# A macaron hybrid block on one core: the opening's order written out further, weight buffers kept for blocks, activation sums split late

## The chip, the cores and the metric

The kernel runs on one core of one Trainium2 chip. The metric is the device time of one execution in microseconds (us), as the median of several runs; less is better. TensorE (PE) multiplies matrices and holds a stationary operand that a separate weight load (PEld) brings in; ScalarE (ACT) and VectorE (DVE) work element by element; SyncE (SP) only issues the DMAs of the weights here.

## The reference

One layer over x of 256 positions by 2048 features, in float32: a half-step SwiGLU FFN, a token mixer of two head groups, a second half-step FFN, and a final norm.

```python
def swiglu_ffn(x, w_gate, w_up, w_down):
    return (jax.nn.silu(x @ w_gate) * (x @ w_up)) @ w_down
...
x = x + 0.5 * swiglu_ffn(rms_norm(x, ffn1_norm), ffn1_w_gate, ffn1_w_up, ffn1_w_down)
z = rms_norm(x, mix_norm) @ w_in
...
x = x + y @ w_out
x = x + 0.5 * swiglu_ffn(rms_norm(x, ffn2_norm), ffn2_w_gate, ffn2_w_up, ffn2_w_down)
return rms_norm(x, final_norm)
```

The FFN's inner width is 5632 (11 chunks of 512), the mixer reads 5120 columns of w_in. All weights are float32 and are read once: 340 MB. The change touches the two FFNs only.

## The kernel before

**Three matmuls for one.** TensorE's operands are fp32r. Each float32 operand is kept as two parts, hi (the value rounded by a cast on ScalarE) and lo (the rest, a subtraction on VectorE), and a product is hi·hi + lo·hi + hi·lo. A *unit* is a weight tile of 512 rows by 512 columns (1 MB, 128 partitions by 4 by 512). `unit` (L207) loads it into a raw buffer, casts it in two halves (`hi`, two ACT instructions of 128x1024) and subtracts (`lo`, one DVE instruction of 128x2048). `multiply` (L214) runs the unit against the activations of both position tiles: 16 matmuls with the hi part, then 8 with the lo part.

**Seven products for eight.** `seven` (L379) computes a block of two row units by two column units of a weight with seven products of 12 matmuls (Strassen's scheme in Winograd's form); the remaining rows of the block are `usual` units of 24. The weight sums of the scheme (w11 = w12 − w11, then w22 − w11, and so on) are VectorE subtractions in place, in the raw buffers; a product's own hi and lo parts are made from the sum. The activations' sums are made once for each set of blocks by `seven_of` (L349): four sums of which each is split into hi and lo, numbered 4, 5, 6 and 2 by the product that uses them. The products run in the order 0, 4, usual, 5, usual, 6, 2, usual, 3, usual, 1. After the first two, `snap` copies their banks to SBUF on ScalarE (s1, s5), after the third and fourth again (u2, u3).

**An FFN.** `ffn` (L440) first multiplies the first 512 columns of gate and up unit by unit, while it normalises the activations. Then come five steps s, each with one gate and one up block of 1024 columns (`seven` at L761 and L763). After steps 0, 2 and 4, `down` (L686) turns the hidden chunks made so far into an update of the residual: a `product` of plain units for output columns 0 (c = 0), the sums of the hidden activations by `seven_of`, a `seven` block for columns 1 and 2, and a `product` for columns 3. The first of these has three row units, the others four. So there are six down blocks and twelve down products in the two FFNs.

**What sets the order.** Each engine executes its own queue in order. The queues are laid out at build time by the tile framework's planner: it goes through the instructions in program order, and where the next one isn't ready by its own reckoning, it takes a later one that is. An instruction issued through the `Engine` wrapper (L32) while `Engine.pinned` is true is kept behind the pinned ones before it on its engine; later ones that aren't pinned may still pass it. The opening of the first FFN (`begin`, L561, the first 512 columns of gate and up while x and the weights come in) is pinned and written out by hand, and the pin holds on until `meanwhile(0)` (L753), that is, until s1 and s5 of the first gate block are issued. SP's queue is kept in program order (`sp.held`) through that first block.

**The opening.** x comes in by chunks of 512 columns, the first in two halves. Two norm-free activation units are made first: each 128 columns of x are turned by TensorE (`norm.turn`, two transposes), scaled and cast by ScalarE, subtracted by VectorE. The first gate unit comes in four quarters; `products(j)` (L586) is the quarter's six matmuls. In the loop of L595 each pass issues a turning, the quarter's cast and subtraction, and the products of the pass before. Five idle matmuls stand ahead of it (`keep_busy(5)`, two weight loads each), and two more behind the first transposed vector.

**Buffers.** Weight tiles come into three `raw` buffers (L179) or two `kept` ones (L177). The kept ones hold w11 and w12 of a block (L389). In the first FFN's steps and from there on, two of every five plain units of the down products take a kept buffer too (L173 to L175). Split tiles (hi and lo) have two sets and a third for every third unit. Thirteen small `keep` tiles hold the copies and the activation sums.

Of the kernel before, what the change touches and what calls it, by code (L numbers as in the profile page):

```python
# [13 lines left out]
ALU = mybir.AluOpType  # L14
# [35 lines left out]
def hybrid_block(ctx: ExitStack, tc: tile.TileContext, a: dict, out: bass.AP):  # L50
# [52 lines left out]
    early = const.tile([P, 1], F32, name="early")  # L103
    act.activation(early, ones[:, :1], AF.Copy, scale=1.0)

# [29 lines left out]
    first_turn()  # L135
    keep_busy(2)
    pe.held = False
# [31 lines left out]
    extra = []  # L169
    turn_of = {"raw": 0, "split": 0, "hold": False}  # L170

    def load(src, name, pieces=((0, UK),), loaded=None, kept=False):
        if kept is None and extra and not turn_of["hold"]:  # L173
            turn_of["raw"] += 1
            kept = turn_of["raw"] % 5 > 2  # L175
        if kept:
            raw = extra[0].tile([P, UK, CW], F32, tag="kept", name=f"raw_{name}", bufs=2)  # L177
        else:
            raw = raws.tile([P, UK, CW], F32, tag="raw", name=f"raw_{name}")  # L179
        for i, e in pieces:  # L180
            sp.dma_start(raw[:, i:e, :], src[i * P : e * P].rearrange("(j p) c -> p j c", p=P))
            if loaded:
                loaded(i)
        return raw
# [22 lines left out]
    def unit(src, name):  # L207
        return parts_of(load(src, name, kept=None), name)

# [22 lines left out]
    class Norm:  # L232
# [4 lines left out]

        def squares(self, c):
            for t in range(NT):
# [109 lines left out]
    def seven_of(sf, x0, x1, v, spare, parts):  # L349

        a11, a12, a21, a22 = v[0, 0], v[0, 1], v[1, 0], v[1, 1]
        parts = iter(parts)

        def split(i, q):
            hi, lo = next(parts)
            act.copy(hi, q)
            dve.tensor_tensor(lo, q, f32(hi), op=ALU.subtract)
            sf[i] = [(hi[:, j, :], lo[:, j, :]) for j in range(UK)]  # L360

        sf.update({0: stationary(x0, 0), 1: stationary(x1, 0), 3: stationary(x1, 1)})
        dve.tensor_tensor(spare, a21, a22, op=ALU.add)
        split(4, spare)
# [9 lines left out]
        return rest  # L374

    def quad(tile):
        return tile.rearrange("p (j c) -> p j c", j=UK)

    def seven(w, rows, cols, sf, xs, name, keep, done, between=None):  # L379

# [38 lines left out]
        product_of(5, w11, a)  # L419
# [20 lines left out]
    def ffn(tag, norm, after, opening=False):  # L440
        with tc.tile_pool(name=f"ffn{tag}", bufs=1, side="left") as fp:
            extra.append(fp)
            turn_of["hold"] = True
            wg, wu, wd = (a[f"ffn{tag}_w_{s}"][0] for s in ("gate", "up", "down"))
# [87 lines left out]
            def sums():  # L532
# [5 lines left out]
                else:  # L538
                    left.pop()()

# [15 lines left out]

            def joint(u, m, blk, middle=None, late=None):
                x = norm.xT[u] if u < 2 else units[u]
                multiply([(ps[m, t], stationary(x, t), u == 0, u % 2 == 1) for t in range(NT)], blk, True, middle, late)

            def begin():  # L561
# [16 lines left out]

                def mm(u, m, middle=None, late=None):
                    joint(u, m, blocks(*parts[u, m]), middle, late)  # L580

# [34 lines left out]
                high(1, "g")  # L616
                norm.squares(1)
                norm.squares(2)
                low(1, "g", ends)
                plain(1)  # L620
                mm(1, "g")
# [12 lines left out]
                mm(1, "u", norm.rows, lambda: turn_both(2))  # L634
                low(2, "g")
# [46 lines left out]
            if not opening:  # L682
                first_hidden()
            turn_of["hold"] = False

            def down(last):  # L686
# [10 lines left out]
                for c in (0, 3):  # L697
# [8 lines left out]
                    if c == 0:  # L706
                        sh = {}
                        seven_of(
                            sh, hidden[m], hidden[n],
                            {(t, i): turned[u, t] for t in range(NT) for i, u in ((0, m), (1, n))},  # L710
                            quad(keep(f"hspare{tag}_{m}")),
                            [[quad(keep(f"hs{tag}_{m}_{i}_{z}", F32R)) for z in range(2)] for i in range(4)],
                        )()
                        got = {}
# [7 lines left out]
                        if tag == 1 and m == 5:  # L722
                            prepare()
                        seven(wd, (m, n), (2 * CW, CW), sh, [(u, hidden[u]) for u in us[:-2]], f"d{tag}_{m}", keep, add)
                hidden.clear()
                turned.clear()

            for s in range(5):
# [31 lines left out]

                seven(wg, (0, 1), cs, sf, xs, f"g{tag}_{s}", keep, gate, meanwhile)  # L761
                sp.held = False
# [348 lines left out]
```

## Time and profile before

| | us |
|---|---|
| median of 3 runs | 1738.01 |
| lowest and highest | 1737.01, 1739.35 |
| the profiled execution's own time | 1736.9 |
| its span, first to last instruction | 1735.1 |
| TensorE busy, matmuls | 1721.8 |
| VectorE busy | 1477.9 |
| ScalarE busy | 1046.9 |

The profile is one execution; its times count from the start of the span. A row of the timeline has the start, the length from the first to the last of a run of like instructions, the engine, the source line (nearly all are L43, the wrapper's, so one goes by the tile names), the operation, out<-in, the shape, how many, and in brackets the engine's idle time before it and what ended it. The names: raw, hi and lo with _g, _u, _d for gate, up and down, with _p in a product of the seven, with _x in a usual unit; xs and hs are the split activation sums, ps the banks. PEld rows are weight loads; one precedes each matmul.

### The profile page before, as it was taken

To read this page: it belongs to the slowest core of one execution; us is meant where nothing else is said; L and a number is where in the kernel's file an instruction comes from. 1 tells how busy PE (TensorE), PEld (TensorE's weight loads), DVE (VectorE), ACT (ScalarE), POOL (GpSimd) and SP (SyncE) were. 2 spreads that over 40 slices of the span, in tenths; PEclk is the share of its full clock that TensorE was granted. 3 is DMA by queue.
4 is the path that set the end of the run, shared out by engine and by line. 5 is a ranking of instruction groups with operands and counts; after the bars stand their busy time and mean duration, and the time that the engine had idled before them with its cause. 6 is when DMAs were issued, how large, how long until landed. Compare 5 with 4: busy or idle time off the path is not lost. (4 is left out here: it accounts for less than half of the span.)

```text
span 1735.1 us, 20339 instructions
## 1 busy us (share of the span) xinstructions
PE 1721.8 (99%) x8045; PEld 1437.0 (83%) x8045; DVE 1477.9 (85%) x1213; ACT 1046.9 (60%) x1354; POOL 6.9 (0%) x32
## 2 busy tenths in 40 slices
PE   9999999999999999999999999999999999999998
PEld 7788888888888888888888888888888888888886
DVE  7998989889789888687986669989799887899895
ACT  8666565656466656565655546656556664556654
POOL 1000000000000000000000000000000000000000
PEclk9999999999999999999999999999999999999999
DMA  8663665666466656555555763575475646555743
GB/s 281 209 225 136 217 220 193 198 239 218 149 212 204 205 182 213 174 169 194 180 186 187 246 210 130 195 242 189 166 251 195 214 143 225 194 194 195 255 172 107
DMA packets 174224, 343.24 MB, mean 198 GB/s; under 512 B 5684, under 2 KB 8624, under 8 KB 174000
## 3 DMA queue, kind: packets, MB, share of 16 engines
q1 hardware_dynamic: 173632, 340.81, 58.2%
q8 instruction: 63, 1.03, 0.2%
q10 hardware_dynamic: 176, 1.06, 0.1%
q14 instruction: 33, 0.27, 0.0%
q0 software_dynamic: 320, 0.07, 0.0%
HBM read 339.82 MB, written 2.10 MB: 197 GB/s over the span
## 5 line engine op out<-in xcount | busy, mean ns | idle before, releaser
L43 ACT CAST hi_g_p<-raw_g 128x1024 fp32r<-128x1024 f32 x140 | 142.5, 1050 | 104.3 <-DVE raw_g L43 27.3
L43 DVE TENSOR_TENSOR lo_g_p<-raw_g,hi_g_p 128x2048 fp32r<-128x2048 f32 x70 | 159.4, 2287 | 33.4 <-ACT hi_g_p L43 33.3
L43 ACT CAST hi_u_p<-raw_u 128x1024 fp32r<-128x1024 f32 x140 | 141.2, 1049 | 69.9 <-PE ps_u_a L43 24.4
L43 DVE TENSOR_TENSOR lo_u_p<-raw_u,hi_u_p 128x2048 fp32r<-128x2048 f32 x70 | 159.1, 2286 | 18.8 <-ACT hi_u_p L43 18.5
L43 PE MATMUL ps_d<-hi_d,h 128*128 128x512 f32 x704 | 168.0, 390 | 0.0
L43 PEld LDWEIGHTS ps_d<-hi_d,h 128*128 128x128 f32 x704 | 131.5, 188 | 27.0
L43 PE MATMUL ps_in<-xT_nm,hi_in 128*128 128x512 f32 x640 | 153.3, 391 | 0.0
L43 PEld LDWEIGHTS ps_in<-xT_nm,hi_in 128*128 128x128 f32 x640 | 117.4, 188 | 23.2 <-ACT tha L43 0.3
L43 ACT CAST hi_d<-raw_d 128x1024 fp32r<-128x1024 f32 x88 | 88.3, 1049 | 67.9 <-PE ps_u_d L43 22.4
L43 DVE TENSOR_TENSOR lo_d<-raw_d,hi_d 128x2048 fp32r<-128x2048 f32 x44 | 100.6, 2291 | 30.8 <-ACT hi_d L43 30.8
L43 DVE TENSOR_TENSOR lo_in<-raw_in,hi_in 128x2048 fp32r<-128x2048 f32 x40 | 91.4, 2286 | 39.1 <-ACT hi_in L43 38.5
L43 ACT CAST hi_in<-raw_in 128x1024 fp32r<-128x1024 f32 x80 | 80.0, 1045 | 67.4 <-PE ps_in L43 45.9
L43 ACT CAST hi_d_p<-raw_d 128x1024 fp32r<-128x1024 f32 x84 | 84.4, 1048 | 51.7 <-DVE raw_d L43 39.4
L43 ACT CAST hi_g_x<-raw_g 128x1024 fp32r<-128x1024 f32 x80 | 81.3, 1048 | 49.6 <-PE ps_g_c L43 24.8
L43 DVE TENSOR_TENSOR lo_d_p<-raw_d,hi_d_p 128x2048 fp32r<-128x2048 f32 x42 | 95.4, 2287 | 11.9 <-ACT hi_d_p L43 11.8
L43 ACT CAST hi_u_x<-raw_u 128x1024 fp32r<-128x1024 f32 x80 | 80.5, 1047 | 34.1 <-PE ps_u_c L43 20.2
L43 DVE TENSOR_TENSOR raw_u<-raw_u,raw_u 128x2048 f32<-128x2048 f32 x40 | 91.6, 2289 | 8.6 <-DMA raw_u<-in_ffn_w_up_dram 8.0
L43 DVE TENSOR_TENSOR raw_g<-raw_g,raw_g 128x2048 f32<-128x2048 f32 x40 | 91.4, 2288 | 8.2 <-DMA raw_g<-in_ffn_w_gate_dram 7.6
L43 DVE TENSOR_TENSOR lo_g_x<-raw_g,hi_g_x 128x2048 fp32r<-128x2048 f32 x40 | 91.4, 2286 | 7.1 <-ACT hi_g_x L43 6.9
L43 DVE TENSOR_TENSOR lo_u_x<-raw_u,hi_u_x 128x2048 fp32r<-128x2048 f32 x40 | 91.4, 2285 | 1.1 <-ACT hi_u_x L43 1.0
L43 PE MATMUL ps_d<-lo_d,h 128*128 128x512 f32 x352 | 87.3, 389 | 0.0
L43 PEld LDWEIGHTS ps_in<-xT_nm,lo_in 128*128 128x128 f32 x640 | 82.1, 191 | 3.1
(363 smaller groups left out, 3565.4 us busy)
## 6 DMA issues: line engine op xcount, KB each, us to landing
raw_d<-in_ffn_w_down_dram SPq DMA_DIRECT2D x88, 1024.0 KB, 5.1
raw_u<-in_ffn_w_up_dram SPq DMA_DIRECT2D x87, 1024.0 KB, 5.2
raw_g<-in_ffn_w_gate_dram SPq DMA_DIRECT2D x86, 1024.0 KB, 5.3
raw_in<-in_w_in_dram SPq DMA_DIRECT2D x40, 1024.0 KB, 5.1
raw_o<-in_w_out_dram SPq DMA_DIRECT2D x16, 1024.0 KB, 5.1
xres<-in_x_dram SPq DMA_DIRECT2D x3, 512.0 KB, 9.4
raw_g<-in_ffn_w_gate_dram SPq DMA_DIRECT2D x4, 256.0 KB, 5.8
raw_u<-in_ffn_w_up_dram SPq DMA_DIRECT2D x2, 512.0 KB, 8.1
```

The costliest lines, as they stand in the source:

```text
L43: ins = getattr(self.engine, name)(*args, **kwargs)
```

## The change

Six edits:

1. The first ScalarE instruction is a Sqrt instead of a Copy; two idle matmuls are gone.
2. The opening's loop issues the quarter products in pairs, after every second turning. x's second chunk is loaded behind the second half of the first up unit, its third behind the second gate unit.
3. In the three units that follow, casts, subtractions and squares go by halves in another order, and the hi matmuls run over the first two row groups of both position tiles ahead of the last two. The turning of x's second chunk moves inside the first up unit (`within`).
4. The pin of the opening reaches to u2, the copy behind the first gate block's third product. The last two pairs of activation sums are made at written places in that block: the sums behind the first product's parts, the splits of 5 and 6 around w11's first sum, the last sum and split 2 behind u2. There, w22 − w11 is issued ahead of the usual unit (`early`).
5. Plain units take `raw` buffers only.
6. In the down blocks, only sum and split 5 are made ahead of the block. Split 6, the last sum and split 2 come behind the third product's weight sum, ahead of its parts.

```diff
-    act.activation(early, ones[:, :1], AF.Copy, scale=1.0)
+    act.activation(early, ones[:, :1], AF.Sqrt)
...
-    keep_busy(2)
...
     def load(src, name, pieces=((0, UK),), loaded=None, kept=False):
-        if kept is None and extra and not turn_of["hold"]:
-            turn_of["raw"] += 1
-            kept = turn_of["raw"] % 5 > 2
...
-        return parts_of(load(src, name, kept=None), name)
+        return parts_of(load(src, name), name)
...
-    def multiply(targets, blk, apart=False, middle=None, late=None):
+    def multiply(targets, blk, apart=False, middle=None, late=None, pieces=(range(UK),), within=None):
...
-        for ps, st, begin, _ in targets:
-            for j in range(UK):
-                pe.matmul(ps, st[j][0], blk[j][0], start=begin and j == 0, stop=False, **more)
-                pe.matmul(ps, st[j][1], blk[j][0], start=False, stop=False, **more)
+        for js in pieces:
+            for i, (ps, st, begin, _) in enumerate(targets):
+                if within and js is pieces[-1] and i == len(targets) - 1:
+                    within()
+                for j in js:
+                    pe.matmul(ps, st[j][0], blk[j][0], start=begin and j == 0, stop=False, **more)
+                    pe.matmul(ps, st[j][1], blk[j][0], start=False, stop=False, **more)
...
+        def high(i):
+            hi, lo = parts[i]
+            act.copy(hi, quads[i])
             sf[i] = [(hi[:, j, :], lo[:, j, :]) for j in range(UK)]
+        def low(i):
+            hi, lo = parts[i]
+            dve.tensor_tensor(lo, quads[i], f32(hi), op=ALU.subtract)
-        def rest():
+        def two():
             dve.tensor_tensor(a21, a11, a21, op=ALU.subtract)
             dve.tensor_tensor(a11, spare, a11, op=ALU.subtract)
-            split(5, a11)
-            split(6, a21)
+        def last():
             dve.tensor_tensor(a12, a12, a11, op=ALU.subtract)
-            split(2, a12)
...
         product_of(0, w11, a, True)
+        if between:
+            between("first")
         dve.tensor_tensor(w11, w12, w11, op=ALU.subtract)
+        if between:
+            between("first sum")
         product_of(4, w11, c, True)
         s1 = snap(a, "s1")
         s5 = snap(c, "s5")
         if between:
             between(0)
+        if early:
+            dve.tensor_tensor(w11, w22, w11, op=ALU.subtract)
         usual(0, b2, 1, (e, 1, True, not two), (c, 0, False, False))
         if between:
             between(1)
-        dve.tensor_tensor(w11, w22, w11, op=ALU.subtract)
+        if not early:
+            dve.tensor_tensor(w11, w22, w11, op=ALU.subtract)
+        if between:
+            between("sum")
         product_of(5, w11, a)
...
                     norm.turn((j,))
                     high(0, "g", quarters[j : j + 1])
                     low(0, "g", quarters[j : j + 1])
-                    if j:
+                    if j % 2:
                         products(j - 1)
-                products(UK - 1)
-                fetch(0, "u", ends, lambda i: load_x(1) if i == 0 else None)
+                        products(j)
+                fetch(0, "u", ends)
+                load_x(1)
+                fetch(1, "g", ends)
                 load_x(2)
-                fetch(1, "g", ends)
                 load_x(3)
-                high(0, "u")
-                his, los = turn(1)
-                his()
-                norm.squares(0)
-                low(0, "u", ends)
-                los()
-                plain(0)
-                mm(0, "u")
+                js = (range(2), range(2, UK))
+                high(0, "u", ends[:1])
+                norm.squares(0, (0,))
+                low(0, "u", ends[:1])
+                high(0, "u", ends[1:])
+                norm.squares(0, (1,))
+                low(0, "u", ends[1:])
+                def second():
+                    his, los = turn(1)
+                    his()
+                    los()
+                mm(0, "u", None, None, js, second)
...
-                high(1, "u")
-                norm.squares(3)
-                low(1, "u")
+                norm.squares(3, (0,))
+                high(1, "u", ends[:1])
+                norm.squares(3, (1,))
+                low(1, "u", ends[:1])
+                high(1, "u", ends[1:])
                 norm.factor()
                 norm.diagonals()
+                low(1, "u", ends[1:])
...
-                        )()
+                        )
+                        two()
+                        high(5)
+                        low(5)
+                        def others(i):
+                            if i == "sum":
+                                high(6)
+                                low(6)
+                                last_sum()
+                                high(2)
+                                low(2)
...
                     if opening and s == 0:
-                        Engine.pinned = False
-                        if i:
-                            (sums, first_hidden)[i - 1]()
+                        two, last, high, low = left[0]
+                        if i == "first":
+                            two()
+                            high(5)
+                            high(6)
+                        elif i == "first sum":
+                            low(5)
+                            low(6)
+                        elif i == 2:
+                            Engine.pinned = False
+                            last()
+                            high(2)
+                            low(2)
+                            first_hidden()
```

More of the change, by code (lines that the diff above doesn't have):

```diff
@@ L353, in seven_of, with seven @@
         a11, a12, a21, a22 = v[0, 0], v[0, 1], v[1, 0], v[1, 1]
[L354 to L359, printed above, removed]
+        parts = dict(zip((4, 5, 6, 2), parts))
+        quads = {4: spare, 5: a11, 6: a21, 2: a12}
+        sf.update({0: stationary(x0, 0), 1: stationary(x1, 0), 3: stationary(x1, 1)})
+        def high(i):
+            hi, lo = parts[i]
+            act.copy(hi, quads[i])
             sf[i] = [(hi[:, j, :], lo[:, j, :]) for j in range(UK)]
-        sf.update({0: stationary(x0, 0), 1: stationary(x1, 0), 3: stationary(x1, 1)})
-        dve.tensor_tensor(spare, a21, a22, op=ALU.add)
-        split(4, spare)
-        def rest():
+        def low(i):
+            hi, lo = parts[i]
+            dve.tensor_tensor(lo, quads[i], f32(hi), op=ALU.subtract)
+        def two():
             dve.tensor_tensor(a21, a11, a21, op=ALU.subtract)
             dve.tensor_tensor(a11, spare, a11, op=ALU.subtract)
-            split(5, a11)
-            split(6, a21)
+        def last():
             dve.tensor_tensor(a12, a12, a11, op=ALU.subtract)
-            split(2, a12)
-        return rest
+        dve.tensor_tensor(spare, a21, a22, op=ALU.add)
+        high(4)
+        low(4)
+        return two, last, high, low
     def quad(tile):
         return tile.rearrange("p (j c) -> p j c", j=UK)
-    def seven(w, rows, cols, sf, xs, name, keep, done, between=None):
+    def seven(w, rows, cols, sf, xs, name, keep, done, between=None, early=False):
         a, c, e, d = (bank(f"ps_{name}_{n}") for n in "aced")
@@ L538, in sums @@
                 else:
-                    left.pop()()
+                    two, last, high, low = left.pop()
+                    two()
+                    for i in (5, 6):
+                        high(i)
+                        low(i)
+                    last()
+                    high(2)
+                    low(2)
             left = []
@@ L577, in low, with mm @@
                         low_part(*(z[:, i:e, :] for z in [raw[u, m]] + parts[u, m]))
-                def mm(u, m, middle=None, late=None):
-                    joint(u, m, blocks(*parts[u, m]), middle, late)
+                def mm(u, m, *more):
+                    joint(u, m, blocks(*parts[u, m]), *more)
                 def turn(c):
@@ L683, in ffn @@
                 first_hidden()
-            turn_of["hold"] = False
             def down(last):
@@ L707, in down @@
                         sh = {}
-                        seven_of(
+                        two, last_sum, high, low = seven_of(
                             sh, hidden[m], hidden[n],
@@ L759, in meanwhile @@
                         sums()
-                seven(wg, (0, 1), cs, sf, xs, f"g{tag}_{s}", keep, gate, meanwhile)
+                seven(wg, (0, 1), cs, sf, xs, f"g{tag}_{s}", keep, gate, meanwhile, opening and s == 0)
                 sp.held = False
```

30 lines of the change are left out of this document (18 added, 12 removed).

## The prediction, made before the change was run

> **What bounds the kernel now.** I read the page first, then the waits of TensorE's weight loads, the chain of waits and the timeline round each wait. In a wait's row the numbers are the total, how often, and the longest.
>
> ```profile
> PE 1721.8 (99%) x8045; PEld 1437.0 (83%) x8045; DVE 1477.9 (85%) x1213; ACT 1046.9 (60%) x1354; POOL 6.9 (0%) x32
> ```
> ```profile
> PEld ps_d_a L43 <- DVE lo_d_p L43: 2.5, 3, 1.3
> PEld ps_g_a L43 <- ACT hi_g_p L43: 1.4, 4, 0.7
> PEld ps_g_e L43 <- DVE lo_g_x L43: 1.1, 1, 1.1
> ```
> ```profile
> 1441.20 5.44 PE ps_d_a L43 x24
> ```
>
> TensorE is the bound: it is busy for 99% of the span. Where nothing stops it, 24 matmuls of 512 columns take 5.44 us, 0.227 each, and no edit changes their number. So the change can only win waits of TensorE, and those named above are most of them. The weight loads (PEld) show them better than the matmuls, whose modelled ends cover part of a wait. ScalarE (casts: the "hi" parts) and VectorE (subtractions: the "lo" parts, and the sums of the seven-product scheme) matter only where TensorE catches up with them.
>
> The sum is made against the profiled execution, 1736.9 us (span 1735.1 and 1.8 around it). The median of the runs is 1738.0, so 1.1 us are added at the end.
>
> **The start: products in pairs.**
>
> ```profile
> 3.70 0.90 PEld L43 LDWEIGHTS idle<-ones 128*128 128x128 f32 x4
> 7.36 0.62 ACT L43 CAST hi_g<-raw_g 128x512 fp32r<-128x512 f32 x1 [0.95 <-DMA raw_g<-in_ffn_w_gate_dram]
> 8.11 0.20 PEld L43 LDWEIGHTS pt_n<-ident,xres 128*128 128x128 f32 x2 [0.80 <-DMA xres<-in_x_dram]
> 9.56 0.37 PEld L43 LDWEIGHTS pt_n<-ident,xres 128*128 128x128 f32 x2
> 9.90 0.76 PEld L43 LDWEIGHTS ps_g<-hi_g,xT_n 128*128 128x128 f32 x4
> 10.58 0.61 ACT L43 CAST hi_g<-raw_g 128x512 fp32r<-128x512 f32 x1
> 11.24 0.82 PEld L43 LDWEIGHTS ps_g<-hi_g,xT_n 128*128 128x128 f32 x4
> 12.57 1.02 PEld L43 LDWEIGHTS pt_n<-ident,xres 128*128 128x128 f32 x8
> 13.74 1.05 ACT L43 CAST hi_u<-raw_u 128x1024 fp32r<-128x1024 f32 x1 [1.60 <-DMA raw_u<-in_ffn_w_up_dram]
> 14.84 2.59 PEld L43 LDWEIGHTS ps_u<-hi_u,xT_n 128*128 128x128 f32 x12 [0.51 <-ACT hi_u L43]
> 19.28 3.59 PEld L43 LDWEIGHTS ps_g<-hi_g,xT_n 128*128 128x128 f32 x16
> ```
>
> Call T0 to T3 the four turnings of x, P0 to P3 the four quarter products (six matmuls, 1.36 us). Before, TensorE's queue is T0 T1 P0 T2 P1 T3 P2 P3: each turning stands a product ahead of its use. After, it is T0 T1 P0 P1 T2 T3 P2 P3. P1 needs the cast of the second quarter, which waits for its DMA and ends at 7.36 + 0.62 = 7.98, so P1 ends near 9.34 and only then T2 goes. From T3 (9.56) to P3 (11.24), through the scaled copy and the cast behind it (10.58) on ScalarE, the trace has 1.68 us. Put on T2, P2 starts at 11.02 instead of 9.90. P2 and P3 take 2.72, to 13.74. Then comes the up unit with 5.44 and, now inside it, the eight transposes of 1.02: 20.20, where before the next unit began at 19.28. **Cost +0.9.** In it the 0.51 wait for the second half of raw_u is already won: that half is loaded ahead of x's second chunk, one 512 KB transfer earlier. Should ScalarE get T2 sooner, the cost falls to 0; a gain beyond 0.5 has no wait to come from.
>
> Taking away two keep_busy matmuls (four weight loads, 0.90 at 3.70) lets T0 go earlier, but P1 still waits for the DMA: nothing. What they might hide is the clock:
>
> ```profile
> PEclk9999999999999999999999999999999999999999
> 25.69 1.28 ACT L43 ACT_TABLE_LOAD   x1
> 28.48 0.52 PEld L43 LDWEIGHTS pb_n<-diag_n,ones 128*128 128x128 f32 x4 [0.17 <-issue]
> ```
>
> The granted clock is full in every slice, so I price the loss of cover at nothing. [...] The table load that the early Sqrt removes (1.28) is ahead of the norm's factor; TensorE waited only 0.17 for what comes of it: up to −0.1, taken as 0. The halves of casts and subtractions in units 1 keep the order in which TensorE asks for them, and ScalarE has the 1.28 to spare: 0, at most +0.5.
>
> **The first block, pinned through its third product.**
>
> ```profile
> 54.23 1.77 PEld L43 LDWEIGHTS ps_g_a<-hi_g_p,x 128*128 128x128 f32 x8
> 55.84 2.29 DVE L43 TENSOR_TENSOR raw_g<-raw_g,raw_g 128x2048 f32<-128x2048 f32 x1
> 56.14 1.99 ACT L43 CAST hi_g_x<-raw_g 128x1024 fp32r<-128x1024 f32 x2
> 58.04 2.29 DVE L43 TENSOR_TENSOR lo_g_p<-raw_g,hi_g_p 128x2048 fp32r<-128x2048 f32 x1
> 60.80 1.07 PE L43 MATMUL ps_g_c<-lo_g_p,xs 128*128 128x512 f32 x4
> 62.31 0.58 ACT L43 COPY s_g<-ps_g_c 128x512 f32<-128x512 f32 x1
> 62.59 0.30 PEld L43 LDWEIGHTS ps_g_e<-lo_g_x,x 128*128 128x128 f32 x2 [1.15 <-DVE lo_g_x L43]
> 67.24 0.77 PEld L43 LDWEIGHTS ps_g_a<-hi_g_p,xs 128*128 128x128 f32 x4 [0.25 <-ACT hi_g_p L43]
> 68.19 0.76 PEld L43 LDWEIGHTS ps_g_a<-hi_g_p,xs 128*128 128x128 f32 x4 [0.18 <-ACT hi_g_p L43]
> 70.52 0.76 PEld L43 LDWEIGHTS ps_g_a<-lo_g_p,xs 128*128 128x128 f32 x4 [0.19 <-DVE lo_g_p L43]
> ```
>
> Before, this block loses 1.15 + 0.25 + 0.18 + 0.19, less the ordinary 0.04 of each load: 1.6. The planner was free behind the second product, and used it: the casts hi_g_x (56.14) ran ahead of the copy s5 (62.31), and TensorE had the e product to do while VectorE was late. After, `usual(0)` is pinned, so its casts stand on ScalarE's queue **behind** s5, and s5 waits for the end of the second product. Queued behind s5 are both casts of b2, the casts for the third product and u2; for the first of them waits TensorE, whose own queue is pinned too. From the last matmul's end: s5 0.58, half of the casts 1.0, and about 0.4 by which weight loads normally run ahead of a matmul's end: a new wait of 2.0, and 0.1 for the second half. VectorE: the two sums (0.6 each in sequence; before, one of them ran in a gap) stand ahead of w11's sum, so the second product's cast and lo part come 0.6 later; the cast would end at 56.1 + 0.6 and the lo part at 59.0, or 59.9 with the 0.9 from the start. TensorE asks for it 4.53 behind its start (20 matmuls), at 54.23 + 0.9 + 4.53 = 59.7: 0.2. From there both engines are a full product ahead, so the three later waits go. After: 2.3, before 1.6. **Cost +0.7.** The bounds: −1.6, if the copy never holds ScalarE, and +1.9, by the rival below.
>
> **Down blocks: the last sums late.**
>
> ```profile
> 162.80 0.69 DVE L43 TENSOR_TENSOR hs<-u_g,hs 128x512 fp32r<-128x512 f32 x1
> 163.41 2.29 DVE L43 TENSOR_TENSOR raw_d<-raw_d,raw_d 128x2048 f32<-128x2048 f32 x1
> 165.73 5.79 ACT L43 CAST hi_d_p<-raw_d 128x1024 fp32r<-128x1024 f32 x6 [3.07 <-DVE raw_d L43]
> 167.75 6.70 DVE L43 TENSOR_TENSOR lo_d_p<-raw_d,hi_d_p 128x2048 fp32r<-128x2048 f32 x3 [0.51 <-ACT hi_d_p L43]
> 170.10 0.76 PEld L43 LDWEIGHTS ps_d_a<-lo_d_p,hs 128*128 128x128 f32 x4 [1.29 <-DVE lo_d_p L43]
> ```
> ```profile
> 1188.70 0.77 PEld L43 LDWEIGHTS ps_d_a<-lo_d_p,hs 128*128 128x128 f32 x4 [0.57 <-DVE lo_d_p L43]
> ```
> ```profile
> 1677.19 0.76 PEld L43 LDWEIGHTS ps_d_a<-lo_d_p,hs 128*128 128x128 f32 x4 [0.62 <-DVE lo_d_p L43]
> ```
>
> In three of the six down blocks TensorE waits for the lo part of the third product. VectorE was busy up to it: hs, the sum of w11 (163.41), the casts that this sum releases, the lo part. Three VectorE operations of 0.69 (0.6 apart) move behind that sum: low(6), the sum a12 and low(2). The sum then starts 1.8 earlier, and they fill the 2 us in which VectorE waits for the casts (165.7 to 167.75). 1.8 is more than each wait, so all three go: **−2.5**, the sum of the three rows. Their next user is the fourth product, a product and more behind. The two casts that move go into ScalarE's idle 3.07. The keep buffers stay 13: spare and a22 are free in time for s1 and s5. What is late next is VectorE's next lo part, by less than 0.3. Bounds: 0 and −2.5.
>
> **Two buffers for blocks alone.**
>
> ```profile
> 1219.95 2.29 DVE L43 TENSOR_TENSOR raw_g<-raw_g,raw_g 128x2048 f32<-128x2048 f32 x1 [5.00 <-DMA raw_g<-in_ffn_w_gate_dram]
> 1234.03 0.77 PEld L43 LDWEIGHTS ps_g_a<-hi_g_p,xs 128*128 128x128 f32 x4 [0.74 <-ACT hi_g_p L43]
> ```
> ```profile
> raw_d<-in_ffn_w_down_dram SPq DMA_DIRECT2D x88, 1024.0 KB, 5.1
> ```
>
> Before, two in five units of the down products take a "kept" buffer. In the second FFN this kept w12 of the first gate block away: VectorE sat idle for 5.00 us, then was late for the third product. Of the 1.4 us for ACT hi_g_p, 0.43 are the opening's; the other 1.0 are here. With the pair free since the block ahead, w12 lands early: **−1.0**, at worst 0. The price is that all units share three buffers. A buffer's turn is 5.1 (landing) + 2.0 + 2.3 = 9.4 us, and three units last 16.3: 6.9 to spare, so nothing.
>
> **Sum.** +0.9 + 0.7 − 2.5 − 1.0 = −1.9: 1735.0 for an execution like the profiled one, **1736.1** against the median.
>
> **Rivals.**
>
> 1. *The opening loses nothing and the waits all go:* −3.5, with up to −1.5 of the opening's own and of small waits that I left alone: 1733 to 1734.5. For it: the start hangs on DMA landings, so a little earlier landing moves T2 and all behind it. Against: s5 stands ahead of the casts on a pinned queue. 18%.
> 2. *The planner fills VectorE's gap badly.* At 55.84 it put the free subtraction w22 − w12 (2.29) ahead of the lo part. If it does so in the pinned block, in the gap while the second product's casts run, that lo part is 1.2 later and so is all behind it: 1737.3. 20%.
> 3. *The gains don't show:* VectorE is at 85%, and a new order moves the waits to the next lo parts; half of 3.5 is left, with the opening's 1.6 to 2.8: 1738 to 1739. 15%.
> 4. *Slower: three buffers starve the down products.* Place: the second and third unit behind each block, when w11, w12, b2 and w22 of the next block are queued on SP ahead of them. If a unit's transfer comes over 6.9 us late, TensorE stands; half a microsecond in each of the twelve products is +6, less 1.9 of the rest: 1742. Against: no TensorE wait on a weight transfer is in the list now. 12%.
> 5. *The clock:* P1 at half pace is 1.36 more, and T2 stands behind it: 1737.5. 5%. [...]
>
> The forecast itself has 30%, with a range of its own from 1734.0 to 1737.6.
>
> **Chances.** A measurement of this kernel tells about 0.2%, 3.5 us, from no change: the borders are 1734.5 and 1741.5. Faster: rival 1 and a quarter of the forecast, 0.25. Slower: rival 4 and a little of 3, 0.14. The rest, 0.61, lies between. The range takes in all but the far ends of rivals 1 and 4: 1732.2 to 1741.0.
>
> **What would show it.** P2's first weight load near 11 us with a wait for a cast; a wait of about 2 us for hi_g_x near 62, behind the copy s_g; no wait for lo_d_p at the third product of any down block; no 5 us DMA idle of VectorE ahead of the second FFN's first gate block. The forecast is wrong if the opening's casts pass s5, if the waits in the down blocks only move, or if SP holds a unit back.

## The result and the profile after

The changed kernel takes 1740.84 us in the median (1738.95 to 1742.13, 22 runs) against 1738.68 (1736.56 to 1740.48, 22 runs) for the kernel before beside it: a ratio of 1.0013 [1.0007, 1.0019]. It is a little slower, by about 2.2 us, inside the band of 0.2% that the prediction called no change. The forecast was 1.9 us faster, 1736.1.

The profiled execution after takes 1738.95 us (span 1737.1), 2.05 more than the one of before. The starts of four TensorE weight loads cut both into the same stages:

| us | before | after | difference |
|---|---|---|---|
| first gate block starts (`ps_g_a`) | 54.23 | 53.87 | −0.36 |
| first gate block lasts, to `ps_u_a` | 42.03 | 47.81 | +5.78 |
| rest of the first FFN, to `ps_in` | 612.95 | 611.60 | −1.35 |
| mixer | 319.86 | 319.87 | +0.01 |
| second FFN, to the last load | 696.76 | 694.73 | −2.03 |

So the gains behind the opening came, 3.4 us of the 3.5 forecast, and one block of 42 us ate them. The page's first part and the waits of TensorE's weight loads, after:

```profile
PE 1722.2 (99%) x8041; PEld 1440.2 (83%) x8041; DVE 1478.5 (85%) x1214; ACT 1046.0 (60%) x1353; POOL 6.9 (0%) x32
```
```profile
PEld ps_g_c L43 <- DVE lo_g_p L43: 2.4, 1, 2.4
PEld ps_g L43 <- ACT hi_g L43: 2.1, 2, 1.1
PEld ps_g_e L43 <- ACT hi_g_x L43: 2.1, 1, 2.1
PEld idle L43 <- DVE ones L43: 1.1, 1, 1.1
PEld ps_d_a L43 <- ACT u_d L43: 0.4, 2, 0.2
```

The three waits of `ps_d_a` for `lo_d_p` (2.5 us before) are not in the list, nor are those of `ps_g_a` for `hi_g_p` (1.4). In their place stand two waits that happen once each. The timeline of the first gate block after shows where:

```profile
54.62 2.00 ACT L43 CAST hi_g_p<-raw_g 128x1024 fp32r<-128x1024 f32 x2 [1.14 <-DVE raw_g L43]
55.63 0.68 DVE L43 TENSOR_TENSOR v<-v,v 128x512 f32<-128x512 f32 x1
...
56.23 2.28 DVE L43 TENSOR_TENSOR raw_g<-raw_g,raw_g 128x2048 f32<-128x2048 f32 x1
...
58.43 2.28 DVE L43 TENSOR_TENSOR lo_g_p<-raw_g,hi_g_p 128x2048 fp32r<-128x2048 f32 x1
60.64 0.68 DVE L43 TENSOR_TENSOR xs<-v,xs 128x512 fp32r<-128x512 f32 x1
60.77 0.76 PEld L43 LDWEIGHTS ps_g_c<-lo_g_p,xs 128*128 128x128 f32 x4 [2.41 <-DVE lo_g_p L43]
...
62.00 0.59 ACT L43 COPY s_g<-ps_g_c 128x512 f32<-128x512 f32 x1 [4.38 <-PE ps_g_c L43]
62.49 1.99 ACT L43 CAST hi_g_x<-raw_g 128x1024 fp32r<-128x1024 f32 x2
63.59 3.06 PEld L43 LDWEIGHTS ps_g_e<-hi_g_x,x 128*128 128x128 f32 x8 [2.06 <-ACT hi_g_x L43]
...
66.74 3.13 PEld L43 LDWEIGHTS ps_g_c<-hi_g_x,x 128*128 128x128 f32 x8
```

Read it from the casts at 54.62. They end at 56.62, and the lo part could follow there. But VectorE's queue has two later operations ahead of it: the last activation sum (55.63) and w22 − w12 (56.23), which the planner let pass because they were ready. The lo part starts at 58.43, and TensorE has waited 2.41. Then copy s5 (62.00) must wait for that product, the casts `hi_g_x` stand behind s5, and TensorE waits again, 2.06. The third loss is in the lengths: eight weight loads take 3.06 and 3.13 instead of the 1.77 of before. The same 7 us in the view by windows, before and then after (PE, PEld, DVE, ACT and POOL busy, granted clock, DMA share, GB/s):

```profile
62.70:69.70 7.00, 7.00 (x31) 5.49 (x32) 6.37 (x4) 4.08 (x5) 0.00 (x0) 1.00 0.59 167
```
```profile
62.70:69.70 7.00, 6.11 (x15) 4.80 (x16) 6.01 (x4) 5.56 (x6) 0.00 (x0) 0.51 0.25 67
```

15 matmuls instead of 31, with a granted clock of 0.51. From the trace, 14 of them start 0.427 us apart instead of 0.227: 2.8 us. The sum closes: waits 2.41 + 2.06 less the ordinary 0.04 of each, and 2.8, less the 1.6 that the block lost before, is 5.6 of the measured 5.78. Put beside the forecast of +0.7 for this block, the wait for the lo part is 2.2 over its 0.2, and the half pace 2.8 over nothing.

### The profile page after: what moved, and what is told of

Same layout as the page of the kernel before. It is cut to its first block, busy times and chain, and to the rows that moved or that the text cites. A ratio compares the mean times of both kernels' runs of the same rounds, so it can differ in the third digit from the quotient of the medians.

```text
span 1737.1 us, 20348 instructions
## 1 busy us (share of the span) xinstructions
PE 1722.2 (99%) x8041; PEld 1440.2 (83%) x8041; DVE 1478.5 (85%) x1214; ACT 1046.0 (60%) x1353; POOL 6.9 (0%) x32
## 4 chain that ended last, share of the span: by engine, by line
PE 97%; DVE 2%; ACT 0%; DMA 0%; issue 0%; DVEq 0%
PE ps_d L43 14%; PE ps_in L43 13%; PE ps_u_a L43 9%; PE ps_g_a L43 9%; PE ps_u_c L43 6%; PE ps_g_c L43 6%; PE ps_d_a L43 5%; PE ps_o L43 5%; PE ps_u_d L43 5%; PE ps_g_d L43 5%; PE ps_d_c L43 3%; PE ps_g_e L43 3%; PE ps_u_e L43 3%; PE ps_d_d L43 3%; PE ps_g L43 2%; PE ps_u L43 2%
```

## The experiments

Code is shown shortened: calls that have lines of their own are joined by semicolons, and dots stand for lines left out.

**1. The first block undone** (`e1_no_block`): the changed kernel with edit 4 taken back.

```diff
-                        if i == "first": two(); high(5); high(6)
-                        elif i == "first sum": low(5); low(6)
+                        if i == 0: Engine.pinned = False
+                        elif i == 1: sums()
                         elif i == 2:
-                            Engine.pinned = False; last(); high(2); low(2)
                             first_hidden()
...
-                seven(wg, (0, 1), cs, sf, xs, f"g{tag}_{s}", keep, gate, meanwhile, opening and s == 0)
+                seven(wg, (0, 1), cs, sf, xs, f"g{tag}_{s}", keep, gate, meanwhile)
```

> The changed kernel with only its fourth edit undone: the first gate block's activation sums and the pin are as before. Theory A (the first block loses it all: waits of 2.4 and 2.1 us there and 14 matmuls at 0.427 us instead of 0.227, 2.8 us; everything else gains): the block's three losses go, the old waits of about 1.6 us come back, so 1740.8 - 7.2 + 1.6 = 1735.2, 3.5 below the kernel before. Rival B (the slow matmuls come from the two idle matmuls that were taken from the start, not from the block's waits): some matmuls still take 0.427 us, and the time is near 1738. Rival C (the gains behind the opening belong to another order there, not to the edits): no gain over the kernel before, 1738 to 1739.

Measured: 1735.45 us (1738.68 to 1739.33 for before in all comparisons), ratio 0.9981 [0.9972, 0.9989]. The block is 42.07 us long again. Against the changed kernel's 1.0013 that makes edit 4 worth +0.32%, 5.6 us; the intervals are far apart. The loss is the block's, and everything else together gains, so rival C is out. So is B: the idle matmuls are missing here too, and full pace holds from 4.56 us to behind the last matmul: P0's four loads take 0.76 at 5.70, and the mean granted clock of the span is 0.999.

**2. TensorE kept busy in the two waits** (`e2_keep_warm`): the changed kernel with four idle matmuls in each, issued between the second product's hi and lo parts and ahead of the usual unit.

```diff
+        def warm():
+            if early:
+                for _ in range(4):
+                    pe.matmul(d[:, :P], ones, ones, start=True, stop=True, skip_group_check=True)
...
-            multiply([(ps, sf[i], begin, end)], parts_of(raw, f"{name}_p{i}"), True)
+            multiply([(ps, sf[i], begin, end)], parts_of(raw, f"{name}_p{i}"), True, warm if i == 4 else None)
...
+        warm()
```

> The changed kernel with four idle 128x128 matmuls put into each of the first block's two new waits (ahead of the second product's lo part and ahead of the usual unit), into a bank that is written afresh later. Nothing that makes the waits is changed. Theory A with the pace as an effect of the idle time: the waits stay, about 0.6 and 0.3 us of idle time in place of 2.4 and 2.1, every matmul behind them takes 0.227 us, and the time falls by 2.8 to about 1738.0. Rival (the pace comes from something else, such as the three engines reading together): 14 matmuls still take 0.427, and the time stays at 1740.8.

Measured: 1738.72, ratio 0.9998 [0.9989, 1.0007]. The block begins at 56.36 in this profile, 2.49 later than after, so the stretch to look at lies later too. The clock is full there:

```profile
62.00:70.00 8.00, 6.17 (x31) 4.84 (x30) 7.00 (x5) 5.49 (x7) 0.00 (x0) 1.00 0.00 0
70.00:78.00 8.00, 8.00 (x37) 6.64 (x36) 6.71 (x5) 6.91 (x9) 0.00 (x0) 1.00 0.77 262
```

The block takes 45.05 us, 2.76 less than after, with waits of 1.29 and 0.92 around the idle matmuls in place of 2.41 and 2.06: the half pace and nothing else, since the work still waits as long (45.05 is 3.0 above before, and the waits alone give 4.4 − 1.6 = 2.8). The half pace is thus a consequence of the idle time, not a loss of its own.

**3. No fill** (`e3_no_fill`): the pin of all engines kept up to w22 − w12, so that neither sum can pass the lo part.

```diff
                         elif i == 2:
-                            Engine.pinned = False
                             last(); high(2); low(2)
+                        elif i == "w12":
+                            Engine.pinned = False
                             first_hidden()
```

> The changed kernel with the pin kept until the weight sum w22 - w12 is issued, so that neither it nor the last activation sum can go ahead of the second product's lo part. Theory A: that lo part starts when its cast ends, near 56.6, and the wait for it falls from 2.4 to about 0.5 us; the wait of 2.1 behind the copy s5 stays. If one wait of 2.1 alone doesn't slow the matmuls, the time falls by 1.9 + 2.8 = 4.7 to 1736.1; if it does, by 1.9 to 1738.9. Rival (VectorE is late for another reason): the wait stays above 2 us.

Measured: 1744.52, ratio 1.0033 [1.002, 1.0045]. The wait for the lo part falls from 2.41 to 0.63, as expected, but the time rises. Loads with their waits, and the copies:

```profile
61.00 0.76 PEld L43 LDWEIGHTS ps_g_c<-lo_g_p,xs 128*128 128x128 f32 x4 [0.63 <-DVE lo_g_p L43]
62.23 0.59 ACT L43 COPY s_g<-ps_g_c 128x512 f32<-128x512 f32 x1 [2.62 <-PE ps_g_c L43]
...
63.81 0.76 PEld L43 LDWEIGHTS ps_g_e<-hi_g_x,x 128*128 128x128 f32 x4 [2.05 <-ACT hi_g_x L43]
...
72.39 0.58 ACT L43 COPY u_g<-ps_g_a 128x512 f32<-128x512 f32 x1
73.39 1.99 ACT L43 CAST hi_g_x<-raw_g 128x1024 fp32r<-128x1024 f32 x2
74.48 2.83 PEld L43 LDWEIGHTS ps_g_e<-hi_g_x,x 128*128 128x128 f32 x8 [2.60 <-ACT hi_g_x L43]
```

The longer pin did to the second usual unit what the old one did to the first: its casts (73.39) stand behind a copy that waits for a product (u2, 72.39), and TensorE waits 2.60. Half pace follows that wait too: the granted clock is 0.55 from 74.40 to 78.20. So the block is as long as after, 47.88. A further 2.04 appears at 108.47 in the up block, for `hi_u_p`, and makes up most of the 2.6 by which the rest of the first FFN is longer than after.

**4. The same with the casts ahead of s5** (`e4_casts_first`): pin and sums as in 3, and the first usual unit's casts moved.

```diff
         s1 = snap(a, "s1")
+        if early:
+            hi, lo = split_tiles(f"{name}_x01")
+            for h in (slice(0, 2), slice(2, UK)):
+                act.copy(hi[:, h, :], b2[:, h, :])
         s5 = snap(c, "s5")
```

> The same longer pin, and the usual unit's two casts issued ahead of the copy s5. Theory A: both waits go but for about 0.5 us, no matmul is slow, the time falls by 2.4 + 2.1 + 2.8 - 0.5 = 6.8 to about 1734.0, 4.7 below the kernel before and 1 below the kernel with the old first block. Rival (the copy s5 isn't what the casts stand behind): the wait of about 2 us for the first cast of the usual unit stays, near 1736.

Measured: 1741.7, ratio 1.0015 [1.0006, 1.0024]. The wait behind s5 is gone, which shows that the copy ahead of the casts was its cause. The 1734.0 did not come, because the same fault behind u2 took the gain: that wait is 3.25, with one of 1.43 ahead of it and half pace for about 3.4 us behind it (worked out from the granted clock of 0.79 over 70 to 78 us), and the block lasts 47.15.

```profile
61.33 1.80 PEld L43 LDWEIGHTS ps_g_e<-hi_g_x,x 128*128 128x128 f32 x8
...
74.03 3.06 PEld L43 LDWEIGHTS ps_g_e<-hi_g_x,x 128*128 128x128 f32 x8 [3.25 <-ACT hi_g_x L43]
```

**5. The buffers alone** (`e5_buffers`): before with edit 5.

```diff
-        if kept is None and extra and not turn_of["hold"]:
-            turn_of["raw"] += 1
-            kept = turn_of["raw"] % 5 > 2
```

> Before with the two extra weight buffers for blocks alone, nothing else changed. Theory: the waits for a weight buffer in FFN2's first gate block (1.0 to 1.4 us in sum) go and nothing takes their place: about 1737.6 beside 1738.7 for before, ratio 0.9990 to 0.9996, and the kernel behind the opening up to FFN2's end shorter by about 1.2. Rival (three buffers fewer for the other products let transfers starve): FFN2's down products get waits of 1 us or more and the time is 1738.7 or above.

Measured: 1735.72, ratio 0.9982 [0.9973, 0.9991]. The rival is out: the waits named don't appear and no starved product does. The gain is larger than expected, 3.1 us [1.6, 4.7], though its profile shows only 1.3: −0.67 in the second FFN, and −0.64 in the first, where the first down block's wait for `lo_d_p` is 0.54 instead of 1.29 without any late sum. So the two gains overlap in part. A likely part of the larger gain is that the waits in the second FFN's first gate block vary. In the four profiles with the old buffers those above 0.15 sum to 1.6 and 1.5 (before, and experiment 12), 2.3 (experiment 11) and 3.0 (experiment 6). The last one has these rows, beside 0.17, 0.20 and 0.74 in the profile of before:

```profile
1221.39 2.29 DVE L43 TENSOR_TENSOR raw_g<-raw_g,raw_g 128x2048 f32<-128x2048 f32 x1 [5.04 <-DMA raw_g<-in_ffn_w_gate_dram]
...
1229.34 0.77 PEld L43 LDWEIGHTS ps_g_c<-lo_g_p,xs 128*128 128x128 f32 x4 [1.01 <-DVE lo_g_p L43]
...
1231.23 1.69 PEld L43 LDWEIGHTS ps_g_c<-hi_g_x,x 128*128 128x128 f32 x8 [0.19 <-ACT s_g L43]
...
1235.46 0.77 PEld L43 LDWEIGHTS ps_g_a<-hi_g_p,xs 128*128 128x128 f32 x4 [1.42 <-ACT hi_g_p L43]
```

**6. The late sums alone** (`e6_late_sums`): before with edit 6.

```diff
-                        )()
+                        )
+                        two(); high(5); low(5)
+                        def others(i):
+                            if i == "sum": high(6); low(6); last_sum(); high(2); low(2)
```

> Before with the down blocks' last activation sums split late, nothing else changed. Theory: the three waits of the down blocks' first loads for the sum's lo part (2.5 us in sum) go: about 1736.2 beside 1738.7, ratio 0.9983 to 0.9989. Rival (the waits only move to another part of the same block): the time stays within 0.5 us of before, and the down blocks show new waits of the same sum.

Measured: 1736.83, ratio 0.9988 [0.9979, 0.9998]. Two of the three waits go; the last down block keeps one, which is 1.19 instead of 0.62:

```profile
PEld ps_d_a L43 <- DVE lo_d_p L43: 1.2, 1, 1.2
```

The changed kernel and experiments 1 and 9, which have the new buffers as well, have no such row. But the buffers don't settle it, since experiments 7 and 10 have both edits and wait there too, 0.56 and 1.19 (the row is experiment 10's):

```profile
1676.55 0.76 PEld L43 LDWEIGHTS ps_d_a<-lo_d_p,hs 128*128 128x128 f32 x4 [1.19 <-DVE lo_d_p L43]
```

What decides it is open. The theory holds for the other two waits.

**7. The idle matmuls back** (`e7_busy_back`): experiment 1 with `keep_busy(2)` put back.

```diff
     first_turn()
+    keep_busy(2)
```

> The changed kernel without the first gate block's edit, and with the two idle matmuls ahead of the first product put back. Theory (without them the clock comes on late in a part of the executions, at 8.8 to 11.1 instead of 4.5 us, for 1.5 to 2.4 us each time): the clock comes on at about 4.5 us, and the time is about 1 us below that of the same kernel without them (1735.45), 1734.5. Rival (the clock's start is decided by something else): 1735.4 again, and late starts are as likely as without them.

Measured: 1735.20, ratio 0.9979 [0.997, 0.9988]. The time is nearer to the rival's, but its interval of 1.6 us to either side can't tell the two apart. What refutes my theory is that kernels that have the idle matmuls also start late in some profiles: `e6_late_sums`, `e8_held` and `e12_before_again`, three of seven, beside five of seven without them. The pace shows it. Four loads of P0 take 1.35 us in the second profile of before, and 0.76 in the first:

```profile
6.42 1.35 PEld L43 LDWEIGHTS ps_g<-hi_g,xT_n 128*128 128x128 f32 x4 [1.05 <-ACT hi_g L43]
```
```profile
6.08 0.76 PEld L43 LDWEIGHTS ps_g<-hi_g,xT_n 128*128 128x128 f32 x4 [1.09 <-ACT hi_g L43]
```

**8. VectorE alone held** (`e8_held`): casts ahead of s5 as in 4, the pin as in the changed kernel, VectorE kept in program order up to w22 − w12, and the idle matmuls of 7.

```diff
                             Engine.pinned = False
+                            first_hidden()
+                            dve.held = True
                             last(); high(2); low(2)
-                            first_hidden()
```

> The changed kernel with three differences: the first usual unit's casts stand ahead of copy s5, VectorE alone is held in program order from the end of the fixed order up to the sum w22 - w12, so that no later sum goes ahead of the second product's lo part, and the two idle matmuls are back at the start. Theory (the block lost by two waits, of 2.06 behind copy s5 and 2.41 behind two filled-in sums, and by half pace after them): the block has one wait of about 0.6 us, no matmul at half pace, is 41.3 to 42.1 us long instead of 47.8, and the time is 1733.8 to 1735.0. Rival (each pinned queue brings a new wait in the next unit, as it did with copy u2): a wait of 1.3 us or more at 70 to 75 us or beyond, a block of 44 us or more, and 1737 or above.

Measured: 1744.16, ratio 1.0032 [1.0019, 1.0045]. The rival came: a new wait of 6.66 at 80.95, a block of 50.07, and over 1737. The kernel has the same fault in a third place, put there by my own edit:

```profile
74.80 1.09 ACT L43 ACTIVATE sg<-ps_g 128x512 f32<-128x512 f32 x2
75.43 1.29 DVE L43 TENSOR_TENSOR sg<-ps_u,sg 128x512 f32<-128x512 f32 x2
...
78.61 2.28 DVE L43 TENSOR_TENSOR lo_g_x<-raw_g,hi_g_x 128x2048 fp32r<-128x2048 f32 x1
...
80.95 1.35 PEld L43 LDWEIGHTS ps_g_e<-lo_g_x,x 128*128 128x128 f32 x4 [6.66 <-DVE lo_g_x L43]
```

`first_hidden` multiplies an activation that ScalarE, not held, makes at 74.80. On the held queue `lo_g_x` stands behind that multiplication and behind the last sum with its split, and TensorE waits 6.66.

**9. Both gains, with the old start and the old block** (`e9_no_start_no_block`): before with edits 5 and 6.

> Before with the two extra buffers and the late sums, without the new start and without the first block's edit. Theory (the two gains add up and the start is worth nothing either way): about 1735.4, as the changed kernel without the block's edit has it (1735.45), ratio 0.9976 to 0.9984. Rival A (the new order of the start costs the 0.9 of the prediction): 1734.5. Rival B (the new order of the start gains 0.4 or more): 1735.9 or above.

Measured: 1733.86, ratio 0.9974 [0.9965, 0.9983]: the fastest version, 4.5 us [3.0, 6.1] below before. It leans to rival A, but its interval overlaps that of experiment 7 (0.9979), which has the new start with the same idle matmuls. Their profiles, both at early full pace (P0's four loads take 0.77 and 0.76), do differ: the first gate block begins at 53.48 here and at 54.49 there. But 0.24 of that lies ahead of P0 (6.03 and 6.27), and other early profiles lie the other way: 54.23 and 54.28 with the old start (before, experiment 5), 53.87 and 53.94 with the new one (after, experiment 1).

```profile
53.48 0.64 PEld L43 LDWEIGHTS ps_g_a<-hi_g_p,x 128*128 128x128 f32 x3
```
```profile
54.49 0.64 PEld L43 LDWEIGHTS ps_g_a<-hi_g_p,x 128*128 128x128 f32 x3
```

**10. The held block, mended** (`e10_held_sums`): VectorE held as in 8, the last sum and `first_hidden` issued behind w22 − w12; no idle matmuls.

```diff
                         elif i == 2:
                             Engine.pinned = False
-                            last(); high(2); low(2); first_hidden()
+                            dve.held = True
+                        elif i == "w12":
+                            dve.held = False
+                            last(); high(2); low(2); first_hidden()
```

> The changed kernel with three differences: the first usual unit's casts ahead of copy s5, VectorE alone held in program order from the end of the fixed order to the sum w22 - w12, and the last activation sum with the first hidden parts' products behind that sum, so that VectorE holds nothing that waits for ScalarE's free part. Theory (each loss of the block was an instruction that a fixed queue held back behind one that waited): waits of about 0.6 (second product's lo part) and at most 0.3 each behind it, no matmul at half pace, a block of 41.0 to 42.0 us instead of 47.8, and 1734.5 to 1735.4. Rival (the block cannot be made shorter than before's order made it: another wait of 1.3 us or more takes the place): a block of 43 us or more and 1736.5 or above.

Measured: 1735.93, ratio 0.9985 [0.9976, 0.9994]. The block is as expected: 41.37 us, one wait of 0.64, full clock:

```profile
56.00:97.40 41.40, 41.18 (x182) 33.74 (x181) 37.32 (x24) 28.62 (x34) 0.00 (x0) 1.00 0.55 185
```

The time is not below experiment 1's. Full pace began late in this profile (10.1 us; P1's first four loads, at 8.28, take 1.61), and the up block behind gives the 0.7 back with a wait of 1.12: its second weight lands when VectorE has already waited 2.07 for it. The wait of 1.19 in the last down block (experiment 6) is in this profile too.

```profile
97.82 2.29 DVE L43 TENSOR_TENSOR raw_u<-raw_u,raw_u 128x2048 f32<-128x2048 f32 x1 [2.07 <-DMA raw_u<-in_ffn_w_up_dram]
...
101.25 0.77 PEld L43 LDWEIGHTS ps_u_c<-hi_u_p,xs 128*128 128x128 f32 x4 [1.12 <-ACT hi_u_p L43]
```

So a fixed order as such wasn't the fault; but in this profile the 0.7 that a good one gains in the block turns into a wait for a transfer in the next.

**11. The start alone** (`e11_start_alone`): before with edits 1 to 3.

> Before with the new order of the start alone (products of the first unit in pairs of quarters, the second product in two halves, no idle matmuls, the other table loaded first). Theory (the start is worth nothing that can be measured): within 0.5 us of before, the first gate block's start between 53.9 and 56 us by the moment at which the clock comes on. Rival A (the prediction's +0.9): 0.6 to 1.2 us above before. Rival B (a gain, 0.36 in the profiles with an early clock): 0.3 us or more below before.

Measured: 1739.14, ratio 1.0 [0.9992, 1.0009], −1.4 to +1.6 us: no difference that can be measured, as the theory had it, but with rival A inside the interval. The first gate block starts at 56.20, just beyond the 56 that was expected for a late clock; full pace came at 10.8 us (two loads at 9.63 still take 0.76, and at 13.12 they take 0.42).

**12. Before again** (`e12_before_again`): the same instructions as before.

> The kernel before in the changed kernel's text, with the same instructions in the same order: a second look at before. Theory (before's own executions differ by the clock's start, 4.5 to 11 us, and by the waits for a weight buffer in the second network's first gate block, 0.9 to 2.4 us): ratio 1.000 within its interval, and a profile in which these two places differ from the first one's. Rival: the profile repeats the first within 0.3 us at each of these places.

Measured: 1738.44, ratio 0.9998 [0.9989, 1.0007]. Full pace comes at 9.8 us instead of 4.5 (P0's four loads take 1.35 instead of 0.76), and the first gate block starts at 55.08 instead of 54.23. The other half of the theory isn't borne out by this profile: the waits for `hi_g_p` sum to 1.4 in both. The waits of that block are larger in two other kernels that keep the old buffers (experiment 5).

## Why the prediction was wrong

- **The first block, +0.7: here it failed**, at +5.6 to +5.8. The wait behind s5 was forecast at 2.0 and measured at 2.06, by the mechanism given (experiment 4 removes it). The step that failed is the one for VectorE: "the cast would end at 56.1 + 0.6 and the lo part at 59.0 ... 0.2". The cast ended at 56.62, but the lo part at 60.71. I counted the operations that the written order puts ahead, and left what the planner puts there to rival 2, at 20% and +1.2. It put two operations there, 2.28 and 0.68, and the wait was 2.41; experiment 3, in which they can't go there, brings it down to 0.63. A pin keeps pinned instructions in order; it doesn't keep unpinned ones out, and TensorE, whose order was now fixed, could no longer do the e product meanwhile.
- **What nothing in the prediction had:** two waits of 2.4 and 2.1 with 1.2 us of work between them were followed by half pace (a granted clock of 0.51), 2.8 us more. Experiment 2, with idle matmuls in both, keeps 1.00. I had looked for the clock at the start only, and dismissed it with a view in which a slice is 43 us wide; the slices after are all 9 as well, with 6.8 us of half clock in them.
- **The start, +0.9:** −0.36 in the profiles, and the times don't decide it (experiment 11). Counted from P0's first load, the first gate block comes 48.2 later in the three early profiles with the new order (after, experiments 1 and 7) and 47.5, 47.9 and 48.2 later in those with the old one (experiments 9 and 5, before). So the order does cost 0.1 to 0.8, but two details were wrong. The second quarter's DMA, on which P1 hung, landed late only in the profiled execution: after, P1 follows P0 directly, at 6.91, and P2 starts at 9.97, not 11.0. And the idle matmuls were not free: without them P0 starts at 5.62 instead of 6.08, behind a first transposed vector at 3.48 in both profiles. The prediction put that gain at nothing.

```profile
6.91 0.88 PEld L43 LDWEIGHTS ps_g<-hi_g,xT_n 128*128 128x128 f32 x4
...
9.97 0.76 PEld L43 LDWEIGHTS ps_g<-hi_g,xT_n 128*128 128x128 f32 x4 [1.09 <-ACT hi_g L43]
```

- **Late sums, −2.5: right for the profile after.** All three waits are gone there; alone the edit gives −2.1 [−3.6, −0.3]. The third comes back, with 0.56 to 1.19, in three of the ten profiles that have the edit (experiments 6, 7 and 10).
- **Buffers, −1.0: right in kind, too small.** Alone −3.1 [−4.7, −1.6]; together with the late sums −4.5. The 6.9 us of room for three buffers held: rival 4 did not occur.
- **Rival 5, the clock at the start:** the two profiles compared above are both early ones, so it had no part in their difference. The forecast's 1.36 for P1 at half pace was my estimate; in the runs P1's first four loads take 1.61 in experiments 2, 3, 8, 10 and 11, and 0.88 after. The late start happens in kernels with and without the idle matmuls. What it costs depends on the order: in the late profiles the first gate block starts at 55.08 and 55.51 with the old start and between 55.40 and 56.44 with the new one.

## What to carry to other kernels

When an order is fixed by hand, look at every pinned instruction that waits for another engine (a copy out of a bank, a multiplication of an activation) and at all that stands behind it on its queue; and remember that a partly pinned queue still lets others in ahead. A stall of TensorE can cost more than its length: after, the two waits of 2.41 and 2.06 were followed by half pace, which took another 2.8 us. A wait on a transfer seen in one profile has one execution's size: compare a second profile before pricing it.

## What the runs showed of the hardware

- In the profiles of after and of experiments 3, 4 and 8 the granted clock fell within the first gate block, during or just behind a wait of TensorE's weight loads. The waits are from the timeline, the clock is from the view by windows:

| profile | waits of the loads (us) | granted clock |
|---|---|---|
| before | 1.15 at 62.59 | 1.00 from 62.7 to 69.7 |
| after | 2.41 at 60.77, 2.06 at 63.59 | 0.51 from 62.7 to 69.7 |
| experiment 2 | 1.29 at 63.27, 0.92 at 66.09 | 1.00 from 62 to 70 |
| experiment 3 | 0.63 at 61.00, 2.05 at 63.81 | 1.00 from 62 to 70 |
| experiment 3 | 2.60 at 74.48 | 0.55 from 74.4 to 78.2 |
| experiment 4 | 1.43 at 70.01, 3.25 at 74.03 | 0.79 from 70 to 78 |
| experiment 8 | 6.66 at 80.95 | 0.57 from 78 to 86 |

- After, half pace lasted from 62.78 to 69.61, 6.83 us. In experiments 3 and 4 it lasted about 3.4 us and in experiment 8 about 6.9, estimates from the granted clock of the stretches in the table.
- What a wait must be like for half pace to follow is not shown: in experiment 3 it followed a wait of 2.60, and did not follow one of 2.05 with 0.63 ahead of it.
- Full pace begins between 4.4 and 5.1 us in six profiles and between 8.8 and 11.1 in eight, at 4.5 and 9.8 in before and experiment 12, which have the same instructions. P0's four loads take 0.76 or 0.77 in the six and 1.35 or 1.36 in the eight.
- What makes a start early or late is not shown. The 0.9 us of idle matmuls did not decide it: three of the seven profiles with them start late, and five of the seven without.
